# Moving the short sequence's recurrence of the last head pair from stage 3 to stage 4

## The chip, the cores and the metric

The kernel runs on one core of a Trainium2 chip. The metric is device time in microseconds (us); lower is better. The core's engines are PE (TensorE matmuls), DVE (VectorE), ACT (ScalarE), POOL (GpSimd) and SP, whose queue issues almost every DMA.

## What is computed

One encoder layer for two sequences, 512 and 256 tokens long, laid one after the other in 768 columns. The mixer, cut to the part that matters here, is a RWKV-7 recurrence over 8 heads, forward and backward in time, a GLA branch that is not touched by the change, and an output projection:

```
def step(S, inp):                       # rwkv7_scan, per head
    r_t, w_t, k_t, v_t, kk_t, a_t = inp
    sa = einsum('bhij,bhj->bhi', S, -kk_t)
    S = S * w_t[:, :, None, :] + sa[..., None] * (kk_t * a_t)[:, :, None, :] + v_t[..., None] * k_t[:, :, None, :]
    return S, einsum('bhij,bhj->bhi', S, r_t)

y = y_f + y_b                           # both directions
gn = group_norm(y) * lnx_w + lnx_b
out = (gn + bonus) * g                  # g: the gate, a small LoRA product
mixed = concatenate([out, gla]);  x = x + rms_norm(mixed @ w_out)
```

Cross attention and a feed-forward block follow. The result is x for both sequences.

## The kernel before

**Chunks and places.** The scan is done in chunks of 64 tokens. The 8 heads make 4 pairs (0 to 3). The long sequence has 8 chunks, the short one 4, and forward and backward run side by side: step j of the forward direction and of the backward one form one `step`. For every pair there are six "places", each with the operands of two such steps: places 0 and 1 hold the first half of the long sequence, 2 and 3 its second half, 4 and 5 the short sequence. `products(st, g)` fills place g: its loads (`bkg<-bkd`, `ard`, `ttd`, `vtd`), small matmuls (`sca`, `scb`), four masked copies on DVE (L1021 to L1024), transposes (`bktp`) and their copies on ACT (L1029).

**One step.** `step(st, x, j, pc)` does step j of part x (0: first half of the long sequence, 1: its second half, 2: the short sequence) in one PSUM bank `rec`. Its links depend on each other: matmuls L1046, copy `rh` on ACT (L1047), matmuls L1059, copies on ACT (L1061), state matmuls L1066, on DVE L1068 and L1074 (the next state), then the next step. L1051 and L1077 make the output y, which DVE (L1086 to L1092) adds into `ya`. Only x = 1 needs what another part made (the end state of x = 0).

**Stages.** `stage(q)` runs for q = 0 to 4. It interleaves, step by step, x = 1 of pair q-1 with x = 0 and x = 2 of pair q: three independent recurrences in stages 1 to 3, two in stage 0, and in stage 4 only x = 1 of pair 3. I number the stages as the code does: stage 3 is the "fourth", stage 4 the "fifth". During a stage the products of later places are made too.

**`finish(st, seqs)`** takes the finished `ya` of a pair: head sums on PE (`hsum`, L639), DVE L1104, square on ACT (L1106), head sums, Ln and Exp on ACT (L1107, L1109), DVE L1110, the load of the bonus, DVE L1112, the load of the gate, DVE L1114. For pairs 0 to 2 one buffer `fb` serves as the square and then takes both loads, one after the other; the result goes to DRAM (`mixd<-ya`) and is read back as `raw<-mixd`. `finish(sts[2])` stands behind stage 3 in the code, `finish(sts[1])` behind stage 2. For pair 3 the bonus and the gate have buffers of their own and the result is split in place into `mix_lsb`, without DRAM. After the mixer's planes, w_out is loaded in 32 pieces (`raw<-in_w_out_dram`) and split on ACT (L149) and DVE (L150); the output projection's matmuls are `po` (L249).

**What sets the order.** A list scheduler gives every engine one program order at build time, by priorities (`tc.high_priority(offset=...)`) and its own estimates of time. On the chip every engine takes its list in that order; so does SP with its DMA issues.

Of the kernel before, what the change touches and what calls it, by code (L numbers as in the profile page):

```python
# [20 lines left out]
SEQS = ((0, 512), (512, 256))  # L21
# [11 lines left out]
def kernel(ctx: ExitStack, tc: tile.TileContext, I, y_prompt, y_sample):  # L33
# [6 lines left out]
    def dma(out, in_):  # L40
        return nc.sync.dma_start(out=out, in_=in_)  # L41
# [36 lines left out]
    def psc(name):  # L78
        return ps.tile([P, 512], F32, tag="c", bufs=3, name=name)
# [65 lines left out]
    def split(hi, lo, src, lo_eng=None):  # L145
        if lo_eng is pool:
            pool.tensor_copy(out=hi, in_=src)
        else:
            act.activation(out=hi, in_=src, func=AF.Copy)  # L149
        (lo_eng or pool).tensor_tensor(out=lo, in0=src, in1=hi, op=ALU.subtract)  # L150
# [164 lines left out]
    def cvc(name, i=0):  # L315
        return cv[:, col[name] + i:col[name] + i + 1]
# [318 lines left out]
    def head_sums(src, fn, psf=psn, seqs=SEQS):  # L635

        for c0, n in seqs:
            pt = psf("hsum")
            pe.matmul(out=pt[:, 0:n], lhsT=ones_bd, rhs=src[:, c0:c0 + n], start=True, stop=True)  # L639
            fn(c0, n, pt)  # L640
# [177 lines left out]
    sts = []  # L818
# [275 lines left out]
    def finish_tile():  # L1094
        return mp.tile([P, D], F32, tag="sxf", name="fb")[:, 0:T]

    def finish(st, seqs=SEQS, tiles=None, mixed=None):

        p, pa = st["p"], st["ya"]
        pb, bon, gt = tiles or (finish_tile(),) * 3  # L1100
        a, b = seqs[0][0], seqs[-1][0] + seqs[-1][1]
        a, b = min(a, seqs[-1][0]), max(b, seqs[0][0] + seqs[0][1])
        cs = slice(a, b)
        head_sums(pa, lambda c0, n, pt: dve.scalar_tensor_tensor(  # L1104
            out=pa[:, c0:c0 + n], in0=pt[:, 0:n], scalar=-1.0 / 64, in1=pa[:, c0:c0 + n], op0=ALU.mult, op1=ALU.add), psm, seqs)
        act.activation(out=pb[:, cs], in_=pa[:, cs], func=AF.Square)  # L1106
        head_sums(pb, lambda c0, n, pt: act.activation(  # L1107
            out=pb[:, c0:c0 + n], in_=pt[:, 0:n], func=AF.Ln, bias=eps_gn, scale=1.0 / 64), psm, seqs)
        act.activation(out=pb[:, cs], in_=pb[:, cs], func=AF.Exp, scale=-0.5)  # L1109
        dve.scalar_tensor_tensor(out=pa[:, cs], in0=pa[:, cs], scalar=cvc("lnx_w", p), in1=pb[:, cs], op0=ALU.mult, op1=ALU.mult)  # L1110
        dma(bon[:, cs], bond[p][:, cs])
        dve.scalar_tensor_tensor(out=pa[:, cs], in0=bon[:, cs], scalar=cvc("lnx_b", p), in1=pa[:, cs], op0=ALU.add, op1=ALU.add)  # L1112
        dma(gt[:, cs], lora[p, 4][:, cs])
        dve.tensor_tensor(out=pa[:, cs], in0=pa[:, cs], in1=gt[:, cs], op=ALU.mult)  # L1114
        if mixed:
            split(mixed[0][:, cs], mixed[1][:, cs], pa[:, cs], dve)
        else:
            dma(mixd[p], pa)
# [35 lines left out]
    def prods(p, gs):  # L1154
        if 0 <= p < 4:
            with tc.high_priority(offset=3000):
                for g in gs:
                    products(sts[p], g)

    def stage(q):  # L1160

        jobs = []
        if q:
            jobs.append((sts[q - 1], 1))
        if q < 4:
            sts[q]["ya"] = yas[q % 3]
            jobs += [(sts[q], 0), (sts[q], 2)]
        pcs = [psc("rec") for _ in jobs]
        for j in range(4):
            with tc.high_priority(offset=4000):  # L1170
                for (st, x), pc in zip(jobs, pcs):
                    step(st, x, j, pc)
            if j % 2:
                if q:
                    prods(q, (2 + j // 2,))
                prods(q + 1, (j // 2, 4 + j // 2))
# [6 lines left out]
    yas += [gdp.tile([P, T], F32, tag="gd", bufs=2, name=f"ya{i}") for i in range(2)]  # L1183
    prods(0, (0, 4, 1, 5))
    stage(0)
    prods(0, (2, 3))
    begin(3)
# [3 lines left out]
    for b in range(16):  # L1191
        memory_block(mem, b)
    mq2_cm.__exit__(None, None, None)
    stage(1)
    with tc.high_priority(offset=2000):
        finish(sts[0])
    joined(3)
    for q in (2, 3):
        stage(q)
        with tc.high_priority(offset=2000):  # L1200
            finish(sts[q - 1])
# [9 lines left out]
    mix = {k: (planes[2 * i], planes[2 * i + 1]) for i, k in enumerate(order)}  # L1211
    mo = [mp.tile([P, T], F32, tag="lsb", bufs=4, name="mo") for _ in range(2)]
    tiles = (finish_tile(), *mo)
    with tc.high_priority(offset=2000):
        finish(sts[3], SEQS[1:], tiles, mix[3])
    stage(4)
    with tc.high_priority(offset=4000):
        finish(sts[3], SEQS[:1], tiles, mix[3])
    for k in order:
        if k != 3:  # L1220
            load_split(mixd[k], *mix[k], lo_eng=pool)
# [264 lines left out]
    with tc.tile_pool(name="f1", bufs=1, reuse_waits="tile") as f1, tc.tile_pool(name="fw", bufs=1, reuse_waits="tile") as fw:  # L1486
# [76 lines left out]
        jobs = [(0, 0), (0, 1), (1, 0), (1, 1)] + [(f, n) for f in (0, 1) for n in range(2, 7)]  # L1563
# [109 lines left out]
        with tc.tile_pool(name="us", bufs=1, side="right", reuse_waits="tile") as us:  # L1673
            acc = [f1.tile([P, D], F32, tag=t, name="acc") for t in ("t2h", "t2l", "t3h", "t3l", "t4h", "t4l")]
            g = us.tile([P, D], F32, name="grow")
            jobs = [(c, n, s_) for c in range(4) for n in range(7) for s_ in (2 * c, 2 * c + 1)]
# [94 lines left out]
```

## Time and profile before

| | |
|---|---|
| median of 3 runs | 1555.07 us (1552.32 to 1568.69) |
| the profiled execution | 1548.75 us, its span 1546.6 us |
| PE busy | 1408.3 us (91%) |
| DVE busy | 1076.7 us (70%) |
| ACT busy | 706.0 us (46%) |
| POOL busy | 220.9 us (14%) |
| SP's DMA queue | 248.54 MB, 53.8% of 16 engines' span |

Every number that is derived below is against the profiled execution, with times counted from the start of its span. Stage 3 runs there from about 700 to 741 us, stage 4 from 741 to 771 us, and the matmuls of the output projection begin at 769 us.

### The profile page before, as it was taken

The numbers are of one execution on the slowest core, as the hardware profiler recorded it, in microseconds if no ns is written. First come the engines' busy times: TensorE is split into PE (matmuls) and PEld (weight loads), VectorE is DVE, ScalarE is ACT, GpSimd is POOL, SyncE is SP. The second block draws the span as 40 slices with busy tenths as digits, with TensorE's granted clock in tenths as the row PEclk, the third lists the DMA queues.
The fourth block names the chain that finished last, engine by engine and source line by source line (L and its number), as shares of the span: only waits on it lengthen the run. The fifth ranks groups of instructions, "written<-read, shape, count | busy, mean of one in ns | idle before, by whom it ended". The sixth has DMA issues, their size and how long they took to land.

```text
span 1546.6 us, 27578 instructions
## 1 busy us (share of the span) xinstructions
PE 1408.3 (91%) x10238; PEld 1183.6 (77%) x10238; DVE 1076.7 (70%) x1913; ACT 706.0 (46%) x1477; POOL 220.9 (14%) x304
## 2 busy tenths in 40 slices
PE   7998899897799987999699999978999999999996
PEld 6886778775676766777478887868999998787785
DVE  5555896698567994866665554279766667788886
ACT  5664345443423442344353454345554555454342
POOL 5301000000000000003211233320000002132132
PEclk9999899987779996799799999988999999999998
DMA  6687666584468667464452332244554547555334
GB/s 165 177 314 210 171 197 156 167 228 102 128 187 232 180 184 168 106 166 144 128 179 98 107 100 79 82 154 155 196 170 153 181 157 291 155 175 172 120 103 136
DMA packets 279562, 250.30 MB, mean 162 GB/s; under 512 B 89264, under 2 KB 227059, under 8 KB 279428
## 3 DMA queue, kind: packets, MB, share of 16 engines
q1 hardware_dynamic: 279428, 248.54, 53.8%
q8 instruction: 81, 1.33, 0.4%
q14 instruction: 53, 0.43, 0.1%
HBM read 164.11 MB, written 82.58 MB: 160 GB/s over the span
## 4 chain that ended last, share of the span: by engine, by line
PE 59%; DVE 13%; DMA 11%; issue 8%; SPq 3%; ACT 3%; POOL 2%; DVEq 0%; ACTq 0%; POOLq 0%
PE pd L249 19%; PE fx L1548 7%; PE gx L1548 6%; PE fz L1548 5%; PE gz L1548 5%; SPq L41 3%; PE po L249 3%; DMA wraw<-in_w_in_dram 1%; DVE ws L1488 1%; PE hsum L639 1%; DVE wl L1539 1%; DMA raw<-in_w_out_dram 1%; PE xo L249 1%; POOL rs L1264 1%; PE bktp L1028 1%
## 5 line engine op out<-in xcount | busy, mean ns | idle before, releaser
L249 PE MATMUL pd<-hT_hi,whi 128*128 128x256 f32 (+1 forms) x512 | 183.5, 358 | 9.1 <-DVE gd L327 4.1
L249 PE MATMUL pd<-hT_lo,whi 128*128 128x256 f32 (+1 forms) x512 | 180.2, 352 | 0.3 <-DVE hT_lo L208 0.3
L249 PE MATMUL pd<-hT_hi,wlo 128*128 128x256 f32 (+1 forms) x512 | 178.5, 350 | 0.0
L149 ACT ACTIVATE whi<-wraw 128x256 fp32r<-128x256 f32 x192 | 77.5, 415 | 97.2 <-PE pd L249 59.4
L249 PEld LDWEIGHTS pd<-hT_hi,whi 128*128 128x128 f32 x512 | 100.9, 197 | 24.0 <-DVE gd L327 4.0
L150 DVE TENSOR_TENSOR wlo<-wraw,whi 128x256 fp32r<-128x256 f32 x192 | 80.2, 437 | 48.2 <-ACT whi L149 46.6
L249 PEld LDWEIGHTS pd<-hT_lo,whi 128*128 128x128 f32 x512 | 101.0, 197 | 13.1 <-DVE hT_lo L208 0.5
L249 PEld LDWEIGHTS pd<-hT_hi,wlo 128*128 128x128 f32 x512 | 100.2, 196 | 13.2 <-issue 0.5
L150 DVE TENSOR_TENSOR ul<-ur,uh 128x768 fp32r<-128x768 f32 x56 | 75.3, 1351 | 30.2 <-ACT uh L149 17.7
L149 ACT ACTIVATE uh<-ur 128x768 fp32r<-128x768 f32 x56 | 47.2, 845 | 106.6 <-PE gz L1548 51.8
L1538 ACT ACTIVATE wh<-w 128x1024 fp32r<-128x1024 f32 x64 | 67.1, 1053 | 36.7 <-PE fz L1548 24.2
L1539 DVE TENSOR_TENSOR wl<-w,wh 128x1024 fp32r<-128x1024 f32 x56 | 68.2, 1217 | 15.3 <-ACT wh L1538 14.7
L1548 PE MATMUL gx<-wh,uh 128*128 128x512 f32 x192 | 74.9, 397 | 4.2 <-DVE acc L1741 4.2
L1548 PE MATMUL gx<-wl,uh 128*128 128x512 f32 x192 | 75.9, 395 | 0.0
L1548 PE MATMUL gx<-wh,ul 128*128 128x512 f32 x192 | 75.4, 395 | 0.0
L1539 POOL TENSOR_TENSOR wl<-w,wh 128x1024 fp32r<-128x1024 f32 x8 | 20.9, 2610 | 329.3 <-ACT wh L1538 329.3
L1548 PE MATMUL fz<-hh,wh 128*128 128x384 f32 x192 | 66.1, 344 | 1.7 <-ACT wh L1538 1.7
L1548 PE MATMUL fz<-hl,wh 128*128 128x384 f32 x192 | 65.9, 343 | 0.0
L1548 PE MATMUL fz<-hh,wl 128*128 128x384 f32 x192 | 65.2, 344 | 0.6 <-DVE wl L1539 0.6
L1538 ACT ACTIVATE wh<-ws 128x1024 fp32r<-128x1024 f32 x48 | 50.5, 1052 | 27.2 <-PE fx L1548 22.5
L1548 PE MATMUL gz<-wl,uh 128*128 128x512 f32 x144 | 56.9, 395 | 0.0
L249 PE MATMUL pd<-mem_hi,wlo 128*128 128x512 f32 x128 | 56.0, 439 | 0.9 <-DVE wlo L150 0.9
(537 smaller groups left out, 3980.4 us busy)
## 6 DMA issues: line engine op xcount, KB each, us to landing
w<-in_w_ff_dram SPq DMA_DIRECT2D x64, 512.0 KB
ur<-ud SPq DMA_DIRECT2D x56, 384.0 KB
wraw<-in_w_in_dram SPq DMA_DIRECT2D x108, 128.0 KB
ud<-u SPq DMA_DIRECT2D x32, 384.0 KB
ud<-us SPq DMA_DIRECT2D x24, 384.0 KB
wraw<-in_wkv_x_dram SPq DMA_DIRECT2D x64, 128.0 KB
lora<-lo_t SPq DMA_DIRECT2D x20, 384.0 KB
bkg<-bkd SPq DMA_DIRECT2D x24, 256.0 KB
```

The costliest lines, as they stand in the source:

```text
L41: return nc.sync.dma_start(out=out, in_=in_)
L149: act.activation(out=hi, in_=src, func=AF.Copy)
L150: (lo_eng or pool).tensor_tensor(out=lo, in0=src, in1=hi, op=ALU.subtract)
L249: pe.matmul(out=out, lhsT=a, rhs=b, start=(i == 0), stop=(i == n - 1))
L639: pe.matmul(out=pt[:, 0:n], lhsT=ones_bd, rhs=src[:, c0:c0 + n], start=True, stop=True)
L1028: pe.transpose(out=pt[:, u, :], in_=fl(b_[HS[h], u]), identity=ident[HS[h], HS[h]])
L1264: pool.tensor_tensor(out=rs, in0=ms, in1=neg_half, op=ALU.pow)
L1488: dve.tensor_tensor(out=out, in0=a, in1=b, op=ALU.subtract)
L1538: act.activation(out=hi, in_=t[name], func=AF.Copy)
L1539: lo_eng.tensor_tensor(out=lo, in0=t[name], in1=hi, op=ALU.subtract)
L1548: pe.matmul(out=out, lhsT=a, rhs=b, start=first and i == 0, stop=last and i == n - 1, skip_group_check=True)
```

## The change

x = 2 of pair 3 is taken out of stage 3's list of jobs and put into stage 4's. `finish` of pair 3, which was called for the short sequence ahead of stage 4 and for the long one behind it, is called for both behind it, the long one first.

```
@@ def stage(q)
         jobs = []
         if q:
             jobs.append((sts[q - 1], 1))
+        if q == 4:
+            jobs.append((sts[3], 2))
         if q < 4:
             sts[q]["ya"] = yas[q % 3]
-            jobs += [(sts[q], 0), (sts[q], 2)]
+            jobs += [(sts[q], 0), (sts[q], 2)][:1 if q == 3 else 2]
...
     tiles = (finish_tile(), *mo)
-    with tc.high_priority(offset=2000):
-        finish(sts[3], SEQS[1:], tiles, mix[3])
     stage(4)
     with tc.high_priority(offset=4000):
-        finish(sts[3], SEQS[:1], tiles, mix[3])
+        for seq in SEQS:
+            finish(sts[3], (seq,), tiles, mix[3])
```

Up to stage 3 every engine's order is the same as before; behind the output projection only a few rows change places. Three places tell what moved.

PE in the third step of stage 3, before. `rec_8159` is the bank of pair 2's second half, `rec_8160` that of pair 3's first half, `rec_8161` that of pair 3's short sequence; `hsum_8139` belongs to `finish` of pair 1:

```order
L1051 MATMUL rec_8159<-pl_hl_4889,pl_hh_4888 64x64 x4
L1059 MATMUL rec_8159<-rh_8385,pl_hl_4889 64x64 x4
L1046 MATMUL rec_8160<-pl_hl_4889 64x64 x4
L1077 MATMUL rec_8161<-pl_hh_4888 64x64 x4
L1028 MATMUL bktp_8132<-ident_80,bkg_8097 128x64 x4
L639 MATMUL hsum_8139<-ya1_4893,ones_bd_85 128x512
L1066 MATMUL rec_8159<-pl_hh_4888,pl3_4890 64x64 x4
L1051 MATMUL rec_8160<-pl_hl_4889 64x64 x4
L1059 MATMUL rec_8160<-rh_8418,pl_hl_4889 64x64 x4
L1046 MATMUL rec_8161<-pl_hl_4889 64x64 x4
```

The same place now:

```order
L1051 MATMUL rec_8159<-pl_hl_4889,pl_hh_4888 64x64 x4
L1059 MATMUL rec_8159<-rh_8326,pl_hl_4889 64x64 x4
L1028 MATMUL bktp_8132<-ident_80,bkg_8097 128x64 x4
L639 MATMUL hsum_8139<-ya1_4893,ones_bd_85 128x512
L1051 MATMUL rec_8160<-pl_hl_4889 64x64 x4
L1059 MATMUL rec_8160<-rh_8359,pl_hl_4889 64x64 x4
L1066 MATMUL rec_8159<-pl_hh_4888,pl3_4890 64x64 x4
```

The short sequence's rows are gone from between those of the two long parts.

DVE in stage 4, before, where `finish` of pair 2 (`ya2`, `fb_8602`) meets the steps of pair 3 (`rec_8655`):

```order
L1110 SCALAR_TENSOR_TENSOR ya2_5890<-ya2_5890,cv_110,fb_8602 128x768
L1068 TENSOR_TENSOR t1_8712<-rec_8655,pcs_5560 128x128
L1074 TENSOR_TENSOR pl_hh_4888<-t1_8712,old_8699 64x2x64 x2
L1055 TENSOR_TENSOR old_8732<-pl_hh_4888,pcs_5560 64x128
L1091 TENSOR_TENSOR ya0_4892<-rec_8655,ya0_4892 128x2x64
L1055 TENSOR_TENSOR old_8732<-pl_hh_4888,pcs_5560 64x128
L1092 TENSOR_TENSOR ya0_4892<-rec_8655,ya0_4892 128x2x64
L1112 SCALAR_TENSOR_TENSOR ya2_5890<-fb_8602,cv_110,ya2_5890 128x768
L1114 TENSOR_TENSOR ya2_5890<-ya2_5890,fb_8602 128x768
```

The same place now, where `rec_8526` is pair 3's second half and `rec_8527` its short sequence:

```order
L1110 SCALAR_TENSOR_TENSOR ya2_5890<-ya2_5890,cv_110,fb_8488 128x768
L1068 TENSOR_TENSOR t1_8609<-rec_8526,pcs_5560 128x128
L1074 TENSOR_TENSOR pl_hh_4888<-t1_8609,old_8596 64x2x64 x2
L1068 TENSOR_TENSOR t1_8642<-rec_8527,pcs_5560 128x128
L1055 TENSOR_TENSOR old_8662<-pl_hh_4888,pcs_5560 64x128 x2
L1091 TENSOR_TENSOR ya0_4892<-rec_8526,ya0_4892 128x2x64
L1074 TENSOR_TENSOR pl_hl_4889<-t1_8642,old_8629 64x2x64 x2
L1092 TENSOR_TENSOR ya0_4892<-rec_8526,ya0_4892 128x2x64
L1089 TENSOR_TENSOR ya0_4892<-rec_8527,ya0_4892 128x128
L1055 TENSOR_TENSOR old_8695<-pl_hl_4889,pcs_5560 64x128 x2
L1112 SCALAR_TENSOR_TENSOR ya2_5890<-fb_8488,cv_110,ya2_5890 128x768
```

Four groups of the short sequence now stand between L1110 and L1112 of `finish` of pair 2.

SP near the end of stage 3, as one piece of the difference (`fb<-bond` and `fb<-lora` are the loads of `finish` of pair 1, the `pl` rows those of pair 3's last place):

```order
 L41 DMA pl_hl<-ttd_761 128x256
+L41 DMA pl_hh<-vtd_765 64x2x128 x2
 L41 DMA fb<-bond 128x768
-L41 DMA pl_hh<-vtd_765 64x2x128 x2
 L41 DMA fb<-lora 128x768
 L41 DMA mixd<-ya_4893 128x768
```

The bonus of pair 1 now stands behind the two loads that refill pair 3's last place.

More of the change, by code (lines that the diff above doesn't have):

```diff
@@ L1164, in stage @@
             jobs.append((sts[q - 1], 1))
+        if q == 4:
+            jobs.append((sts[3], 2))
         if q < 4:
             sts[q]["ya"] = yas[q % 3]
-            jobs += [(sts[q], 0), (sts[q], 2)]
+            jobs += [(sts[q], 0), (sts[q], 2)][:1 if q == 3 else 2]
         pcs = [psc("rec") for _ in jobs]
@@ L1213 @@
     tiles = (finish_tile(), *mo)
-    with tc.high_priority(offset=2000):
-        finish(sts[3], SEQS[1:], tiles, mix[3])
     stage(4)
     with tc.high_priority(offset=4000):
-        finish(sts[3], SEQS[:1], tiles, mix[3])
+        for seq in SEQS:
+            finish(sts[3], (seq,), tiles, mix[3])
     for k in order:
```

## The prediction

> **What bounds the kernel now.** The page first: PE is busy 91% of the span, so the stretches in which it is not are where time can be found.
>
> ```profile
> PE 1408.3 (91%) x10238; PEld 1183.6 (77%) x10238; DVE 1076.7 (70%) x1913; ACT 706.0 (46%) x1477; POOL 220.9 (14%) x304
> ```
>
> Then the busy times in windows of 4 us from stage 3 to the output projection: window, its length, busy us and count of PE, PEld, DVE, ACT and POOL, granted PE clock, DMA share, GB/s.
>
> ```profile
> 732.00:736.00 4.00, 4.00 (x75) 3.21 (x73) 2.47 (x6) 2.61 (x6) 0.00 (x0) 1.00 0.22 66
> 740.00:744.00 4.00, 2.66 (x43) 2.06 (x38) 3.79 (x12) 0.94 (x3) 0.00 (x0) 1.00 0.37 98
> 744.00:748.00 4.00, 4.00 (x30) 2.40 (x28) 1.89 (x6) 0.93 (x3) 0.00 (x0) 0.57 0.27 102
> 756.00:760.00 4.00, 1.57 (x32) 1.11 (x26) 1.02 (x1) 0.82 (x3) 0.00 (x0) 0.71 0.32 94
> 760.00:764.00 4.00, 2.08 (x16) 1.31 (x18) 2.31 (x6) 0.60 (x2) 0.00 (x0) 0.50 0.26 102
> 784.00:788.00 4.00, 3.90 (x17) 2.78 (x16) 2.94 (x7) 3.52 (x9) 0.00 (x0) 1.00 0.80 238
> ```
>
> In stage 3 (first row) PE is full. In stage 4 (756 to 764) it has work for less than half of the time, and DVE is not full either: something is waited for. The chain of waits over 696 to 770 says what (start, us, what):
>
> ```profile
> 745.14 2.02 PE hsum L639 x2
> 747.18 1.06 DVE ya L1104 x2
> 748.27 0.85 ACT fb L1106
> 749.16 1.14 PE hsum L639 x2
> ...
> 751.54 0.74 ACT fb L1109
> 752.31 1.03 DVE ya L1110
> 753.35 3.11 DMA fb<-bond
> 756.49 1.03 DVE ya L1112
> 757.53 3.08 DMA fb<-lora
> ...
> 761.70 2.29 DMA mixd<-ya
> ...
> 766.32 2.68 DMA raw<-in_w_out_dram
> ```
>
> Every row belongs to `finish` of pair 2, not to the recurrence of stage 4. It is a string of links, three of them DMAs of 2.3 to 3.1 us, and at its end hang the weights. SP and PE, in order of time:
>
> ```profile
> 764.05 1.27 SPq L41 DMA_DIRECT2D raw<-mixd  x3
> 765.41 20.15 SPq L41 DMA_DIRECT2D raw<-in_w_out_dram  x30
> 767.84 0.69 PE L1077 MATMUL rec<-pl_hh 128*64 128x64 f32 x8 [1.77 <-ACT pl_hh L1061]
> 769.11 3.02 PE L249 MATMUL po<-w_out,mix_bk 128*128 128x512 f32 x6 [0.57 <-ACT w_out L149]
> 792.39 2.26 PE L249 MATMUL po<-w_pl,mix_lsb 128*128 128x512 f32 x9
> ```
>
> SP can't issue the read-back of pair 2 before `mixd<-ya` has landed, and all w_out loads stand behind it. 30 of them take 20.15 us, so they are paced, and `po` follows them as they come. Stage 4's own last state matmul (767.84) is over before `po` begins and before the weights are there. So the path is: last output of pair 2 in stage 3, `finish` of pair 2, 32 weight loads, `po`. From 776 on PE is full (784 to 788: 3.90 of 4), so what is won ahead of the weights is kept.
>
> **The change part by part.** *Stage 3 loses a third recurrence.* On PE the third step of the short part reads, in the chain of waits:
>
> ```profile
> 728.10 0.38 PE rec L1046 x8
> 729.73 0.38 PE rec L1051 x8
> 730.10 0.23 PE rec L1059 x8
> 732.44 0.38 PE rec L1066 x8
> 734.83 0.38 PE rec L1077 x8
> 736.22 0.38 PE rec L1077 x8
> ```
>
> The first five are the short part, together 1.75 us. A first step lacks L1051 and a last one L1066: 1.37 us each, 6.24 us in all. The sixth row is the last product of pair 2's second half; call its place T. Three of the four short steps stand ahead of T in PE's order: 1.37 + 1.75 + 1.75 = 4.87 us. The second and the third count in full, since PE is full there or waits on DVE, which loses the short part's rows as well (2.05 us a step, below). The first lies where PE waits longest on DVE, for the masked copies of the products, and these stay: I take some 0.8 of its 1.37. So T comes **4.3 us earlier**, at 731.9. The bounds are 2.5 (the third step and the last two rows of the second, 1.75 + 2 x 0.38, which fall after 722) and 4.9 (all).
>
> ```profile
> 728.69 0.59 DVE L1055 TENSOR_TENSOR old<-pl_hl,pcs 64x128 f32<-64x128 f32 x2
> 732.87 0.29 DVE L1068 TENSOR_TENSOR t<-rec,pcs 128x128 f32<-128x128 f32 x1 [1.10 <-PE rec L1066]
> 733.19 0.59 DVE L1074 TENSOR_TENSOR pl_hl<-t,old 64x128 f32<-64x128 f32 x2
> 736.63 1.26 SPq L41 DMA_DIRECT2D pl_hh<-vtd  x2
> 739.15 1.02 DVE L1112 SCALAR_TENSOR_TENSOR ya<-fb,cv,ya 128x768 f32<-128x768 f32 x1 [1.15 <-DMA fb<-bond]
> 743.44 0.94 DVE L1114 TENSOR_TENSOR ya<-ya,fb 128x768 f32<-128x768 f32 x1
> ```
>
> *From T to the square of pair 2 (L1106).* Before, 748.27 - 736.22 = 12.05 us: PE still had the short part's last step, and the head sums started at 745.14 behind it and behind the last transposes. Without them I put the head sums at T + 6 and the two L1104 (1.06 us) at an end of T + 9. But `fb` is one buffer: L1106 may not write it before pair 1's L1114 has read it. Pair 1's bonus load now stands on SP behind the two `vtd` loads (1.26 us), and these wait for T, since they overwrite what T's matmuls read. So: T + 0.5, + 1.3 for `vtd`, + 3.1 and L1112 1.0, + 3.1 and L1114 0.94 (the durations of the same loads above), with half a us of waits on DVE: T + 10.4 to T + 11. I take 11, so **1.05 us** are gained; between 0 and 3 (the head sums alone).
>
> *From the square to the weights.* Before, 765.41 - 748.27 = 17.14 us, nearly all links in series. Now L1109 stands behind two `rh` copies instead of one, and the new rows of the short part stand ahead of L1110 and L1112 on DVE: L1068, L1055, L1074 and two additions, some 0.29 + 0.59 + 0.59 + 2 x 0.29 = 2.05 us a step. A load of 3.11 us hides most of it each time; what sticks out I put at **1.4 us lost**. At the least it is 0; at the most both steps' rows stick out, 4.1. The pair's L1114 stalls DVE until its load lands, as before; one of the two L1068 now stands ahead of it, none did before.
>
> *Stage 4 itself* gains the short part's 6.24 us of PE and 2.05 us of DVE a step. Both recurrences share the waits; PE has them to spare there (1.57 of 4 us at 756). I expect its last state matmul near 763, still ahead of the first weights (761.4 + 2.68 + the split): hidden. Without this cover it would delay the head sums of pair 3.
>
> *The short `finish` behind stage 4.* Its head sums (256 wide) and its ACT and DVE rows stand now among the weight splits and ahead of the first eviction of `po`; the rows below are what they took before, inside stage 4.
>
> ```profile
> 764.77 0.73 DVE L1110 SCALAR_TENSOR_TENSOR ya<-ya,cv,fb 128x256 f32<-128x256 f32 x1 [1.48 <-ACT fb L1109]
> 765.53 0.83 DVE L1112 SCALAR_TENSOR_TENSOR ya<-mo,cv,ya 128x256 f32<-128x256 f32 x1
> 766.40 0.50 DVE L1114 TENSOR_TENSOR ya<-ya,mo 128x256 f32<-128x256 f32 x1
> 794.94 1.29 DVE L1293 TENSOR_TENSOR mo<-po,g_post 128x512 f32<-128x512 f32 x2 [1.80 <-ACT mo L1292]
> ```
>
> With the split that is 2.5 us of DVE in front of an eviction that had 1.80 us to wait anyway, so the eviction comes some 0.7 us later against `po`; PE meanwhile multiplies the next rows into other banks. 0, at most 0.7.
>
> *The rest.* No matmul or transfer is added or dropped; the 32 weight loads keep their pace, 0. A few feed-forward rows change places where PE is full: 0, at most 1 either way.
>
> Sum: -4.3 - 1.05 + 1.4 = **-4 us** (-3.95), that is 1544.8 against the profiled 1548.75. The median of the runs shown, 1555.07, lies 6.3 us higher and its three runs spread by 16; against it the forecast is **1551**.
>
> **The rivals.**
>
> *Given back in stage 4 (20%).* The rows of two recurrences ahead of L1110 and L1112 stick out whole, 4.1 instead of 1.4: -4.3 - 1.05 + 4.1 = -1.3 us, 1554. For it: DVE takes its rows in order. Against it: the links wait for DMAs of 3 us anyway.
>
> *Slower through the clock (12%).* Place: the second half of stage 3. The granted clock falls when PE idles: in 740 to 744 it was busy 2.66 of 4 us, the next window has 0.57, and there the two head sums took 2.02 us (745.14). With two recurrences instead of three PE has less to fill its waits. If the clock halves from about 722 to T, the 10 us of PE work there take 10 more, of which some 1 falls into waits: 9 against -4 gives +5, 1560. It decides from the point at which PE idles for over a third of some 4 us in stage 3. Against it: all windows of stage 3 read 1.00, and products and head sums remain.
> [...]
>
> *A larger gain (10%).* Two recurrences keep PE's clock up in stage 4, where it is 0.50 at 760 to 764: the first six `po` rows (3.02 us, against 2.26 for nine at full clock) save 1.5 us and what follows them until the clock is back some 1 more; pair 1's loads don't hold `fb`, another 2: -8.5, 1546.5.
>
> *It does not do what it says.* The order of ACT has 8 `rh` copies instead of 12 in stage 3 and 8 instead of 4 in stage 4, so this has no share. 8% are left for what I don't see, half on either side.
>
> **How the numbers follow.** The forecast, -4 with its own range from -2 to -6, has 50%. The range that leaves out 2 in 10 goes from -12 to +5 against the median, since a median of three of such runs moves by some us of itself: 1543 to 1560. About 1%, 15.5 us, is what a measurement of this kernel can tell from no change. None of the cases reaches that: faster 0.04, same 0.91, slower 0.05, from the unseen ones and the tail of the clock.
>
> **What would show it.** The last product of pair 2 near 732 instead of 736.2; L1106 of pair 2 near 743 instead of 748.3, right behind pair 1's L1114; the first w_out issue near 761.4 instead of 765.4, and the product with `mix_lsb` near 788.4 instead of 792.4; windows of stage 3 still at 1.00. Wrong would be a first w_out issue at 765 or later, a halved clock ahead of 740, or a stage 4 that ends after the first weights have landed and holds `po`.

## The result: slower by half a per cent, and where the time went

| | before | changed |
|---|---|---|
| median of 20 runs each (lowest to highest), us | 1554.66 (1546.01 to 1575.15) | 1564.61 (1550.81 to 1572.88) |
| profiled execution, its own time, us | 1548.75 | 1571.98 |
| its span, us, and mean granted PE clock | 1546.6, 0.930 | 1570.3, 0.914 |

The ratio of the runs is 1.0053 (95% interval 1.0031 to 1.0075): about 8 us slower where 4 us less were forecast. Comparisons and the counts below leave out runs more than 1.5% above the fastest run of the same kernel (in the counts for the kernel before, four near 1573 us and one of 5610).

The page's first line of the changed kernel, to set beside that of before:

```profile
PE 1429.5 (91%) x10238; PEld 1201.4 (77%) x10238; DVE 1073.0 (68%) x1913; ACT 704.3 (45%) x1477; POOL 219.0 (14%) x304
```

The same 10238 matmuls take PE 21.2 us longer (1429.5 against 1408.3), while DVE and ACT are busy for slightly less. PE's work has not grown; it ran at a lower clock. The windows of the changed kernel say where (same columns as in the prediction: the third number from the end is the granted clock):

```profile
712.00:716.00 4.00, 2.54 (x26) 2.01 (x26) 2.19 (x7) 2.19 (x7) 3.33 (x7) 0.77 0.74 211
716.00:720.00 4.00, 4.00 (x50) 3.66 (x49) 3.12 (x9) 0.98 (x3) 3.16 (x7) 0.50 0.80 237
728.00:732.00 4.00, 4.00 (x41) 3.43 (x40) 2.86 (x11) 0.38 (x1) 0.00 (x0) 0.50 0.16 36
...
742.00:744.00 2.00, 2.00 (x26) 1.71 (x26) 0.77 (x2) 0.54 (x2) 0.00 (x0) 0.50 0.00 0
744.00:746.00 2.00, 1.77 (x24) 0.98 (x26) 1.75 (x7) 0.55 (x1) 0.00 (x0) 0.78 0.02 4
```

At the start of stage 3 PE is idle for 1.46 of 4 us; the clock falls to 0.50 there and stays down for 28 us (716 to 744), nearly the whole of stage 3, though PE reads as busy for 4.00 of 4 us. A PE that reads full is here a PE at half speed, and only the clock's column tells the two apart. Before, the same stretch read 1.00 (732 to 736 in the prediction). The chain of waits of the changed kernel shows the price in single steps, and what follows:

```profile
717.23 0.62 PE bktp L1028 x4
...
720.65 0.62 PE rec L1077 x8
...
740.13 2.00 PE hsum L639 x2
...
750.84 3.62 DMA pl_hl<-ard
...
764.27 0.97 DVE ya L1114
765.26 0.85 ACT fb L1106
...
770.63 3.58 DMA fb<-bond
774.24 1.03 DVE ya L1112
775.28 2.99 DMA fb<-lora
778.37 0.97 DVE ya L1114
779.35 2.29 DMA mixd<-ya
```

Eight L1077 take 0.62 us where they took 0.38 before. The `ard` load of the last place is a link of 3.62 us that the chain of before does not have; that the third recurrence's rows had covered it is likely, but no run shows it. From the square of pair 2 (L1106, 765.26) on the chain has the links of before, with copies of stage 4 on ACT (L1061) and rows on POOL among them. Two ends frame it, the last product of pair 2 (T) on PE and the first weights on SP:

```profile
751.03 0.45 PE L1077 MATMUL rec<-pl_hh 128*64 128x64 f32 x8
783.07 7.11 SPq L41 DMA_DIRECT2D raw<-in_w_out_dram  x9
```

To compare executions, times are counted from the first head sums of pair 0, in stage 2, where the kernels still issue the same work: 674.81 before and 681.64 here. T lies 61.4 us behind them before and 69.4 here, the weights 90.6 and 101.4.

### The profile page after: what moved, and what is told of

Its sections match the earlier page's. It is cut to its first block, busy times and chain, and to the rows that moved or that the text cites. A ratio compares the mean times of both kernels' runs of the same rounds, so it can differ in the third digit from the quotient of the medians.

```text
span 1570.3 us, 27574 instructions
## 1 busy us (share of the span) xinstructions
PE 1429.5 (91%) x10238; PEld 1201.4 (77%) x10238; DVE 1073.0 (68%) x1913; ACT 704.3 (45%) x1477; POOL 219.0 (14%) x304
## 4 chain that ended last, share of the span: by engine, by line
PE 58%; DVE 14%; DMA 12%; issue 7%; ACT 3%; SPq 3%; POOL 2%; DVEq 0%; ACTq 0%; POOLq 0%
PE pd L249 17%; PE fx L1549 7%; PE gx L1549 6%; PE fz L1549 5%; PE gz L1549 5%; SPq L41 3%; PE po L249 2%; DMA wraw<-in_w_in_dram 1%; PE hsum L639 1%; DVE wlo L150 1%; PE xo L249 1%; DVE ws L1489 1%; PE xs L249 1%; PE sca L1017 1%; PE rec L1046 1%
## 5 line engine op out<-in xcount | busy, mean ns | idle before, releaser
L1540 DVE TENSOR_TENSOR wl<-w,wh 128x1024 fp32r<-128x1024 f32 x56 | 68.1, 1217 | 14.7 <-ACT wh L1539 14.2
L1549 PE MATMUL gz<-wh,uh 128*128 128x512 f32 x144 | 56.1, 396 | 1.0 <-ACT uh L149 1.0
```

The costliest lines, as they stand in the source:

```text
L1540: lo_eng.tensor_tensor(out=lo, in0=t[name], in1=hi, op=ALU.subtract)
L1549: pe.matmul(out=out, lhsT=a, rhs=b, start=first and i == 0, stop=last and i == n - 1, skip_group_check=True)
```

## Experiments

Theories. **Clock**: two recurrences leave PE too thin in stage 3; its clock falls there and stays down. **Waits**: the time goes into waits that the third recurrence covered. **Late finish**: the loss is behind stage 4. **Chance**: the fall in the one trace is a bad draw.

### Again, unchanged, and the late finish alone

The third kernel is the one before with only the calls of `finish` moved:

```
-    with tc.high_priority(offset=2000):
-        finish(sts[3], SEQS[1:], tiles, mix[3])
     stage(4)
     with tc.high_priority(offset=4000):
-        finish(sts[3], SEQS[:1], tiles, mix[3])
+        for seq in SEQS:
+            finish(sts[3], (seq,), tiles, mix[3])
```

> The changed kernel once more, for a second trace and more times. Clock theory: with two recurrences stage 3 leaves PE too thin, its granted clock falls there and stays down; this trace again has windows near 0.50 for 12 us or more between the start of stage 3 and the head sums of pair 2, and the ratio to the kernel before stays near 1.005 (+8 us). Wait theory: the time is lost in waits that the third recurrence covered (the last place's products wait for their loads, 3.6 us; pair 2's square waits for pair 1's buffer, 2 us); then these rows are there again and the ratio stays at 1.005 even if the windows of stage 3 read 1.00. Chance: the first trace and its times were a bad draw; the windows of stage 3 read 1.00 as before and the ratio is 1.000 within 0.002.

> The kernel before against itself: what the comparison gives with no change, and a second trace of it. All theories: a ratio within 0.002 of 1. Clock theory: the windows of stage 3 read 0.9 or more again, and its runs at a mean clock of 0.921 take about 1561 us, as those of the changed kernel do. Wait theory: at equal mean clock this kernel is 5 us or more faster than the changed one. Chance: the windows of stage 3 can read 0.50 here as well.

> The kernel before with only the second part of the change: the short sequence's finish of the last pair stands behind stage 4, its recurrence stays in stage 3. Clock theory and wait theory both place the loss in stage 3: ratio 1.000 within 0.002, and windows of stage 3 at 0.9 or more. If the loss is in the late finish itself (its head sums and DVE rows among the weight splits and the first evictions), the ratio is 1.003 or more, with the first eviction of po later by 3 us or more against po's first product.

| kernel | median, us | ratio to before (95%) | runs below a mean clock of 0.9235 |
|---|---|---|---|
| changed, again | 1564.12 | 1.0039 (1.0010 to 1.0069) | 8 of 12 |
| before, again | 1553.48 | 0.9985 (0.9958 to 1.0013) | 1 of 12 |
| before, late finish | 1554.24 | 1.0009 (0.9977 to 1.0041) | 2 of 12 |

The late finish is not the loss. The changed kernel's second trace reads 0.50 in stage 3 as well (728 to 734, and 0.90 from 734 to 736). But the kernel before fell too in its second trace, which took 1567 us (mean clock 0.920):

```profile
708.00:712.00 4.00, 2.38 (x29) 1.69 (x24) 2.30 (x6) 1.96 (x7) 3.37 (x8) 0.85 0.73 205
712.00:716.00 4.00, 4.00 (x45) 3.41 (x45) 3.13 (x8) 1.52 (x4) 2.87 (x7) 0.50 0.82 238
...
746.00:748.00 2.00, 2.00 (x18) 1.21 (x14) 0.86 (x3) 0.82 (x3) 0.00 (x0) 0.50 0.00 0
748.00:750.00 2.00, 2.00 (x49) 1.74 (x48) 1.68 (x6) 1.29 (x3) 0.00 (x0) 0.91 0.04 8
```

So an execution of either kernel can fall, and what differs is how often. Only a few executions have a trace; for all others the mean clock below 0.9235 stands in for the fall. It is a rough sign: the changed kernel's fifth trace fell from 716 to 736 and has a mean of 0.925. All runs with a listed clock, from this section and those below:

| | runs | clock below 0.9235 | their mean, us | mean of the others, us |
|---|---|---|---|---|
| before | 118 | 27 (23%) | 1566.2 | 1554.6 |
| changed | 35 | 25 (71%) | 1566.3 | 1556.8 |

At a like clock the two kernels' times differ by some 2 us at most; the two groups lie 10 to 12 us apart. The share alone makes (0.71 - 0.23) x 11.6 = 5.6 us of the 6.4 us by which the means differ (1563.6 against 1557.2). The expectation of the wait theory, 5 us between the kernels at equal clock, did not come. But among the runs above 0.9235 the changed kernel is not 4 us faster either; it is 2.2 us slower. Of chance one half came: the kernel before can fall too, so the first trace of before was a lucky draw; the ratio did not go to 1.000. The expectation that the kernel before would be at 0.9 or more in its second trace was a miss.

### Filling stage 3 with idle work

A helper puts n matmuls of 128x128 behind the L1046, the L1059 and the L1066 of a step; n = 2 in stage 3:

```
+    def fill():
+        if fills[0]:
+            pt = psd("fill")
+            for i in range(fills[0]):
+                order_after(pe.matmul(out=pt[:, i * P:i * P + P], lhsT=ones_bd, rhs=ident, start=True, stop=True), gate[0])
...
+        fills[0] = 2 if q == 3 else 0
```

> The changed kernel with 44 more matmuls of 128x128 in stage 3, whose results nobody reads: about 6.4 us more PE work at full clock, as much as the short part took away. They wait for nothing but their place in PE's order. Clock theory: PE's clock stays up through stage 3, pair 2's last product comes as early as before or within 2 us of it, and the kernel is faster than the changed one in spite of more work: 1550 to 1556, ratio 0.997 to 1.001. Wait theory: the added matmuls fall partly into waits, nothing else changes: the changed kernel's time or up to 6 us more, ratio 1.005 to 1.009.

Median 1568.13 us, ratio 1.0073 (1.0040 to 1.0107), but no run of 8 below 0.9235, and its stage 3 reads 1.00 both from 716 to 720 and at its end:

```profile
740.00:744.00 4.00, 4.00 (x49) 2.76 (x49) 2.02 (x7) 2.13 (x4) 0.00 (x0) 1.00 0.00 0
```

The clock was held, as the clock theory said; the time it forecast was a miss, and 1.0073 is what the wait theory had expected (1.005 to 1.009). The added matmuls cost all that they saved (0.15 us each was assumed; in the changed kernel with the fill in stage 4, below, one at a clock of 1.00 shows as two records in 0.49 us, and two in 0.71): at full clock the head sums of pair 2 (750.74, 75.6 us behind pair 0's) are hardly earlier than in the four traces in which the changed kernel fell (74.7 to 78.8). This run alone does not decide between the two.

### What tips it: one wait, or the thin stage

In the first trace of the changed kernel, and in the second of before, the fall begins (at 714.16 in the one, between 708 and 712 in the other) behind a wait for block 15's buffer; in the changed kernel's second trace it begins later, behind the masked copies (PE waited 0.55 us for them at 712.27, and eight L1046 at 713.43 still took 0.45 us). PE's rows at that buffer, before and in the changed kernel, in the first traces; the bracket is the idle time ahead and what ended it:

```profile
705.64 0.45 PE L1066 MATMUL rec<-pl 128*64 128x64 f32 x8 [0.96 <-ACT pl L1061]
```

```profile
713.46 0.45 PE L1066 MATMUL rec<-pl 128*64 128x64 f32 x8 [1.90 <-ACT pl L1061]
```

Four kernels: a buffer of its own for block 15 in either kernel (PE's order is unchanged by it), six added matmuls in the first step of stage 3, and the changed kernel without the moved recurrence at all.

```
-        ot = mq2.tile([P, 512], F32, tag="mo", bufs=1, name="mo")
+        ot = mq2.tile([P, 512], F32, tag="mo" if b < 15 else "mo15", bufs=1, name="mo")
```
```
+            fills[0] = 1 if q == 3 and j in (0,) else 0
```
```
-        if q == 4:
-            jobs.append((sts[3], 2))
```

> The changed kernel with a buffer of its own for the last memory block (b = 15), so that the copy at L1136 no longer waits for the store of block 14 (3.4 to 4.3 us in the traces) and PE doesn't stand idle behind it (0.96 to 1.90 us at the start of stage 3). PE's order is the changed kernel's. Clock theory: that idle time is what tips the clock in most runs; without it the windows of stage 3 read 0.9 or more, three runs in four have a mean clock of 0.925 or more, and the median is 1550 to 1555, ratio 0.994 to 1.000. Wait theory: only the idle time itself goes, 1 to 2 us; median 1562, ratio 1.003 to 1.005. If the fall is set by the thin stage alone and not by the idle time, the clock still falls in most runs and the ratio stays at 1.004.

> The kernel before with the same buffer for block 15; PE's order is that of the kernel before. Clock theory: about one run in four of the kernel before has the fall and loses 13 us; without the idle time it has none: mean 3 us lower, ratio of 0.996 to 0.999, and no run above 1561. Wait theory: 1 us less, ratio 0.999.

> The changed kernel with 6 more matmuls of 128x128 in the first step of stage 3 alone, whose results nobody reads; in the run with 44 of them they cost some 0.24 us each on PE, so 1.5 us here. Clock theory: they keep the clock past the place at which it falls; fewer than one run in three has a mean clock below 0.9235, median 1553 to 1557, ratio 0.998 to 1.001. Wait theory: 1.5 us more than the changed kernel, ratio 1.005 to 1.006.

> The changed kernel without the recurrence of pair 3's short sequence (left out, its finish stays and works on other data): two recurrences in stage 3 as in the changed kernel, one in stage 4, 6.2 us less PE work than either kernel. Clock theory: stage 3 is as thin as in the changed kernel, its clock falls in two runs of three, and less work doesn't help: ratio 1.003 to 1.006 over the kernel before, no faster than the changed kernel by more than 2 us. Wait theory: the loss of the changed kernel came from stage 4's second recurrence and its rows among pair 2's finish; without it the ratio is 0.995 to 0.999.

| kernel | median, us | ratio to before (95%) | runs below 0.9235 |
|---|---|---|---|
| changed, own buffer | 1562.37 | 1.0046 (1.0017 to 1.0076) | 8 of 10 |
| before, own buffer | 1552.70 | 0.9985 (0.9953 to 1.0017) | 1 of 12 |
| changed, six matmuls | 1558.85 | 1.0036 (1.0009 to 1.0063) | 2 of 12 |
| changed, short part left out | 1562.65 | 1.0042 (1.0009 to 1.0076) | 9 of 12 |

The first is a miss of the clock theory as I had put it: the one wait is not what tips the clock. Without it the fall came one wait later, in the windows and in PE's row:

```profile
716.00:720.00 4.00, 2.14 (x36) 1.61 (x36) 3.80 (x11) 0.70 (x3) 2.27 (x4) 1.00 0.29 94
720.00:724.00 4.00, 4.00 (x60) 3.65 (x58) 0.80 (x3) 1.50 (x6) 0.00 (x0) 0.51 0.71 231
```

```profile
718.72 0.43 PE L1028 MATMUL bktp<-ident,bkg 64*128 64x64 f32 x4 [1.55 <-DVE pl_hh L1022]
```

PE waits 1.55 us for the masked copies (L1022); with three recurrences the short part's rows stood there. In the kernel before, the own buffer changes nothing that this measurement can tell; that no run would fall was a miss (1564.30 us, its stage 3 at 0.50 from 732 to 736). Six matmuls cut the runs below 0.9235 from 71% to 2 in 12, but 1.0036 lies between the two expectations (0.998 to 1.001 and 1.005 to 1.006), and its interval overlaps that of the changed kernel: what they brought in time is not shown. In its profiled execution (mean clock 0.924) the weights came 92.4 us behind pair 0's head sums, no earlier than before's 90.6. The last is the strongest: with 6.2 us less PE work than either, but two recurrences in stage 3, it falls as often as the changed kernel and is slower than before. The wait theory, which put the loss into stage 4, expected 0.995 to 0.999.

Its profiled execution happened to be at full clock at either end of stage 3 (0.45 us for eight products at 714.33 and at 740.38; at 0.50, at 720.59 in the changed kernel, eight took 0.69), and so sizes the forecast's first term; the two rows under it are the changed kernel's own, from its fourth trace, which read 1.00 from 700 to 736:

```profile
714.33 0.45 PE L1066 MATMUL rec<-pl 128*64 128x64 f32 x8 [1.06 <-ACT pl L1061]
...
740.38 0.45 PE L1077 MATMUL rec<-pl_hh 128*64 128x64 f32 x8
```

```profile
709.35 0.45 PE L1066 MATMUL rec<-pl 128*64 128x64 f32 x8
...
735.65 0.45 PE L1077 MATMUL rec<-pl_hh 128*64 128x64 f32 x8
```

From that L1066 to T it takes 26.1 us, and 26.3 in the changed kernel; before, 736.22 - 705.64 = 30.6; in the changed kernel at half clock 751.03 - 713.46 = 37.6.

### Real work instead of idle work

The products of memory block 15, 24 matmuls of 128x512, are held back into stage 3: 12 behind its first step, 12 behind its second. Nothing is added.

```
-    for b in range(16):
+    for b in range(15):
         memory_block(mem, b)
...
+            if q == 3:
+                held.update({i: gate[0] for i, k in [(0, 0), (12, 1)] if k == j})
+                if len(held) == 2 and j == 1:
+                    memory_block(mem, 15, held)
```

(`held` gives matmuls 0 and 12 of the block the last state matmul of that step to follow.)

> The changed kernel with the 24 products of the last memory block (b = 15) moved into stage 3: 12 behind its first step, 12 behind its second, where PE waited for the masked copies (0.55, 0.73 and 1.55 us of idle time in the traces with two recurrences). No work is added or dropped; the products are 128x512, not 64x64. Clock theory: they fill the place at which the clock falls; at most one run in three has a mean clock below 0.9235, and the median is 1549 to 1556, ratio 0.995 to 1.000. Wait theory: the same work in another place, the waits of stage 4 stay: 1561 to 1565, ratio 1.003 to 1.006. If the end of stage 2 without this block is thin enough to drop the clock there, the fall only moves ahead and the ratio stays above 1.003.

> The kernel before with the same 24 products moved into its stage 3. Clock theory: it falls in one run in four as it is, and with three recurrences there is little idle time to fill: ratio 0.995 to 1.000, and fewer than one run in six below a mean clock of 0.9235. Wait theory: 1.000 within 0.002.

> The changed kernel, one more trace. Clock theory: where the windows of stage 3 read 0.9 or more, the time is 1550 to 1556 and the first w_out load is issued 87 to 91 us after the first head sums of pair 0 (90.6 before at full clock); where they fall to 0.50, 1560 or more and 100 us or more. Wait theory: more than 91 us even at full clock.

The changed kernel with it: 1555.47 us, ratio 0.9982 (0.9957 to 1.0007), 1 of 12 runs below 0.9235, where it had been 71%. The kernel before with it: 1554.70 us, 0.9973 (0.9944 to 1.0001), 2 of 12, where fewer than that were expected. The loss is gone, and no work was taken away. Filled waits alone hardly explain it: in the changed kernel's fourth trace, near 1.00 in stage 3, PE was idle for 2.7 us in all from 704 to 740, and by the medians some 9 us came back. With the kernel that leaves the short part out, this is the main evidence that the falls are the loss. The changed kernel's third trace fell (1563.70 us, weights 101.5 us behind pair 0's head sums), as expected of a fall. The profiled execution of the held kernel, its slowest (1561.38 us, mean clock 0.924, so not among the one in 12), shows that the fall can also move ahead of stage 3, and the way back up:

```profile
692.00:696.00 4.00, 3.53 (x27) 2.60 (x29) 3.41 (x10) 1.45 (x4) 0.98 (x2) 0.53 0.37 109
708.00:712.00 4.00, 4.00 (x40) 3.20 (x37) 2.18 (x7) 1.31 (x4) 0.00 (x0) 0.50 0.39 115
716.00:720.00 4.00, 4.00 (x43) 2.92 (x42) 1.04 (x3) 0.66 (x2) 1.38 (x4) 0.98 0.23 66
```

It fell at the end of stage 2, stayed at 0.50 through small products, and came back right where the held products (from 714 on) stood.

### Was the forecast gain there?

Two more traces each of the held and of the changed kernel, to catch a full clock in stage 3.

> The kernel hold_after once more, for a trace. If its stage 3 keeps a clock of 0.9 or more: in the traces with a full clock there, the time from the first step's L1066 behind block 15's copy to pair 2's last product was 30.6 us with three recurrences and 26.1 us with two; here the last product comes 3 to 5 us earlier against the first head sums of pair 0 than in the kernel before (61.4 us), and the last x1d store at 168 to 171 us (173.0 before). If the gain is given back behind it (the late finish), the last x1d store is at 172 or later though the product came early.

> As for the first look at hold_after: at a full clock in stage 3 pair 2's last product 3 to 5 us earlier than 61.4 us after pair 0's first head sums, and the last x1d store at 168 to 171 us, or at 172 or later if the gain is given back.

> The changed kernel, another trace: one chance in four that stage 3 keeps its clock. Then pair 2's last product 3 to 5 us earlier against pair 0's first head sums than the 61.4 us before, and the last x1d store at 169 to 172 us; if the clock falls, the store at 180 or later.

> The changed kernel, another trace, with the same expectation as the second: at a full clock in stage 3 the last x1d store at 169 to 172 us after pair 0's first head sums, at a fallen one at 180 or later.

Both held ones kept it (1551.38 and 1556.39 us; 1.00 from 728 to 732 in the first, and eight L1077 in 0.45 us at 731.26 in the second). Of the changed ones the second (the fifth in all) fell in full: 1560.48 us, last x1d store at 180.8. The first (the fourth in all) kept 1.00 in most of stage 3, but was at 0.50 ahead of it (692 to 696) and at its end (740 to 744): 1556.99 us, T at 61.4, weights at 94.2 and last x1d store at 176.9, in neither expected range. The first new trace of the held kernel: a window of stage 3 and one of stage 4, then PE, ACT and SP rows:

```profile
728.00:732.00 4.00, 4.00 (x79) 3.07 (x79) 1.37 (x4) 2.71 (x6) 0.00 (x0) 1.00 0.54 164
764.00:768.00 4.00, 3.02 (x30) 2.28 (x29) 1.96 (x4) 2.73 (x8) 3.94 (x8) 0.50 0.54 166
```

```profile
677.21 1.56 PE L639 MATMUL hsum<-ya,ones_bd 128*128 128x512 f32 x4
731.26 0.45 PE L1077 MATMUL rec<-pl_hh 128*64 128x64 f32 x8
743.52 0.84 ACT L1106 ACTIVATE fb<-ya 128x768 f32<-128x768 f32 x1 [3.73 <-DVE ya L1104]
763.15 6.78 SPq L41 DMA_DIRECT2D raw<-in_w_out_dram  x9
846.50 0.99 SPq L41 DMA_DIRECT2D x1d<-res  x2
```

The first and the last of these rows in the kernel before:

```profile
674.81 1.56 PE L639 MATMUL hsum<-ya,ones_bd 128*128 128x512 f32 x4
847.80 0.99 SPq L41 DMA_DIRECT2D x1d<-res  x2
```

And of the kernel before with block 15 held, whose profiled execution also read 1.00 through stage 3:

```profile
681.36 1.56 PE L639 MATMUL hsum<-ya,ones_bd 128*128 128x512 f32 x4
...
744.53 0.45 PE L1077 MATMUL rec<-pl_hh 128*64 128x64 f32 x8
...
776.10 19.56 SPq L41 DMA_DIRECT2D raw<-in_w_out_dram  x30
```

In the held changed kernel T comes 731.26 - 677.21 = 54.0 us behind pair 0's head sums, 7.4 earlier than before's 61.4, where 3 to 5 were expected; the weights 85.9, 4.7 earlier than 90.6; the last x1d store, the end of the output projection, 169.3 against 173.0, 3.7 earlier. But two things differ from before there, the recurrence and block 15. With block 15 held in both, the traces lie further apart: T 63.2, weights 94.7, x1d 177.2 in the held kernel before, whose clock fell behind T (0.50 from 752 to 760). So an earlier T is there when the clock holds; the size of what reaches the weights is not settled. From the store to the end, 703.2 us against 698.8, the gain is gone again in this execution. That stretch differs by some us from execution to execution (698.8 to 704.3 in all; 698.8 to 702.6 in the six traces with the recurrence in its old place, 699.9 to 704.3 in the other 13), and why it is longer here stays open.

Stage 4 still fell (0.50 at 764). So the last pair holds both: block 15 in stage 3 and added matmuls in stage 4, one per place in the changed kernel, two in the kernel before, which has one recurrence there.

```
+        fills[0] = 1 if q == 4 else 0
```

> hold_after with one more 128x128 matmul, whose result nobody reads, at each of three places of a step of stage 4 (23 in all, some 5.5 us of PE time, most of it in waits: in stage 4 PE was busy for 2.1 to 3.0 of 4 us). In all traces so far the clock read 0.50 for 8 us or more between 752 and 784, and the first products of po ran under it. If that fall costs what stage 3 gained, the clock stays up there, the first po rows go at full clock and the ratio falls to 0.994 to 0.998 (2 to 3 us less than hold_after). If po's start is set by the weights alone, 0.998 to 1.000, or up to 2 us more where the added rows stand in front of the chain.

> hold_before with two such matmuls at each place of a step of its stage 4 (one recurrence there, so about as many in all). If the fall in stage 4 costs something, 0.994 to 0.998 here too, and the difference to hold_fill4 is what the moved recurrence is worth with a held clock: by the traces of hold_after with a full clock 3.5 us up to the last x1d store; if the gain is given back behind it, none.

The changed kernel: **1548.46 us, ratio 0.9943 (0.9909 to 0.9976)**, all 12 runs at 1555.39 or less. The kernel before: 1554.15 us, 0.9980 (0.9944 to 1.0015). The first beats both kernels of this study. Between the two the means differ by 6.9 us, with a standard error of 1.9; between the two held ones without the fill by 0.1, with one of 1.3. So whether the moved recurrence gains in the whole time once the clock is held is not settled: only the pair with the fill says so, its two fills are not the same, and three of the second kernel's 11 runs (1561.80 to 1566.10) make 3 of the 6.9 us. The one of these with a trace was at 0.50 in stage 2 (676 to 684), far from the change. How the fill helps is open too: in the profiled execution (1554.63 us, one of the slowest of the 12) stage 4 fell against the expectation, came back only ahead of `po`'s main part, and the last x1d store stood at 174.6, later than before's 173.0:

```profile
756.00:760.00 4.00, 4.00 (x46) 3.32 (x44) 0.96 (x1) 1.10 (x4) 0.00 (x0) 0.50 0.36 98
776.00:780.00 4.00, 4.00 (x18) 3.11 (x17) 2.46 (x6) 2.15 (x6) 0.00 (x0) 1.00 0.39 125
```

## Why the prediction was wrong

- **T comes 4.3 us earlier.** This is the step that failed. The count was right for the clock that the one profile of before showed: between the L1066 of the first step and T it takes 4.3 us less in the changed kernel where its stage 3 kept 1.00 (30.6 to 26.3). But it took that clock as given. With the short part gone the mean clock is below 0.9235 in 71% of the executions instead of 23%; in the profiled one the clock was 0.50 for 28 us and T came 8 us later (69.4 against 61.4).
- **What is won ahead of the weights is kept.** This is not shown either: in the held trace 4.7 us at the weights were 3.7 at the last x1d store and none at the end. That the 4.7 lie near the forecast 4 is luck: T was 7.4 earlier instead of 4.3, and the stretches behind it, for which 0.35 us of loss in all were forecast, lost 2.7.
- **The rival "slower through the clock"** named what happened, and in the changed kernel's profile the fall came at its point of decision: PE idle for over a third of 4 us (2.54 busy of 4, 37% idle). It is no rule: the kernel before with block 15 held was busy for 2.34 of 4 (696 to 700) and stayed at 1.00, and the changed kernel's fifth trace fell after 2.89 of 4 (712 to 716). The rival had the place too late (the second half of stage 3 instead of its first step), the length too short (14 us instead of 28), and the chance at 12%. What spoke for more was on the table: the three times shown for before reach from 1552 to 1569, 1% apart, and the profile, at 1548.75, was one whose stage 3 kept its clock. "All windows of stage 3 read 1.00" was one draw.
- **How long PE waited.** No PE wait in the quoted rows was longer than 1.90 us, and the clock fell behind a stretch in which PE was busy for 1.52 of 3.42 us (last section).
- **From T to the square of pair 2**, 11 forecast: 14.2 in the changed kernel, in part at half clock (0.50 from 756 to 760) and with the `ard` wait of 3.62 us that I had not seen; 743.52 - 731.26 = 12.3 in the held trace, against 12.05 before: nothing was gained here. That pair 1's L1114 would stand right ahead of the square came as said (764.27 and 765.26).
- **From the square to the weights**, 17.14 before, 18.5 forecast: 783.07 - 765.26 = 17.8 in the changed kernel, 19.6 in the held trace.
- **The late finish**, 0 to 0.7: the kernel with that part alone is at 1.0009 (0.9977 to 1.0041), no more than the measurement can tell.
- **"Given back in stage 4" and "a larger gain"** did not come. The chance of "same", 0.91, fits a change of 0.5%, but the sign was wrong and 1564.6 lies outside the range.

## What to carry to other kernels

Read the clock's column beside PE's busy share: a PE full of small products may be full at half speed (here 4.00 of 4 us at 0.50). Before work is taken out of a stage, ask whether it was what kept PE busy between waits; if so, try other real work in its place, as block 15's products here. And where run times of one kernel spread by a per cent, take more than one trace before its clock is taken as given: here the change moved the odds far more than the cost at a like clock.

## What was not expected of the hardware

With PE busy the clock stayed at either level. With small products (64x64 and 128x64 most of all) it stayed at 1.00 in the kernel before (708 to 724, where no 128x512 product ran and PE was busy for 3.31 to 4.00 of 4), and at 0.50 for 28 us in the changed one (4.00 of 4). There it came back only 4 us after the first head sums of 128x512 (from 744 on, where they started at 740.13), and in the second trace of before some 5 us after them (from 748 on, 0.91). Here are these:

```profile
742.64 2.07 PE L639 MATMUL hsum<-ya,ones_bd 128*128 128x512 f32 x2
```

In the held kernel it was back at 716, behind the held 128x512 products. Against that, four such products from 693.05 to 695.1 had not brought it back in the same execution (0.50 from 706 to 716). So PE's busy share alone is not what brings the clock back; what does, no run shows.

The moments at which the clock changed are in the traces too. In the first trace of each kernel (39 changes before, 45 in the changed one) the changes of the granted clock lie whole multiples of one step, 3.413 us, apart. The changed kernel's fall runs from 714.16 to 744.88, nine steps. Its windows cut at such steps, the last two at the way back, and then the one of before that holds the same wait:

```profile
710.74:714.16 3.42, 1.52 (x45) 1.21 (x38) 0.98 (x3) 1.30 (x4) 2.39 (x6) 1.00 0.85 220
714.16:717.57 3.41, 3.41 (x36) 2.72 (x30) 2.79 (x8) 1.48 (x4) 2.74 (x6) 0.50 0.80 249
...
741.46:744.88 3.42, 3.42 (x27) 1.94 (x26) 1.55 (x4) 0.54 (x2) 0.00 (x0) 0.50 0.01 2
744.88:748.29 3.41, 3.08 (x43) 1.99 (x44) 2.46 (x9) 1.90 (x4) 0.00 (x0) 1.00 0.00 0
```

```profile
702.99:706.40 3.41, 2.45 (x73) 2.07 (x72) 1.04 (x3) 1.30 (x4) 3.11 (x7) 1.00 0.78 226
```

With the whole of these two traces cut into such stretches, the clock fell from 1.00 behind all 30 in which PE was busy for less than 0.45 of the stretch, behind 13 of the 57 between 0.45 and 0.80, and behind none of the 683 above. The busy share alone does not give the way back: of 89 stretches at 0.50 with PE busy for 0.80 or more, 41 were followed by a rise. This was counted from the traces afterwards, and no run was made to test what lets the clock fall.
